# Sliding attention's values: split float32r products against plain float32 products at two column positions

## The chip, the core and the metric

The kernel runs on one core of a Trainium2 chip. The metric is the device time of one execution in microseconds (us), taken as the median of several runs. The engines are named as in the profile: PE is TensorE's matrix product, PEld its load of the stationary operand, DVE is VectorE, ACT is ScalarE, POOL is GpSimd, SP is SyncE, which here only issues DMAs.

## The reference

One layer of a decoder trunk on a sequence of 512 tokens of width 1024, all in float32. The part that matters is the sliding-window attention: eight query heads of width 64, two key and value heads, blocks of 128 queries that see their own block of keys and the one before, ALiBi distances, and a learned sink.

```python
sizes = [SWA_Q, SWA_KV, SWA_KV, DIFF_QK, DIFF_QK, DIFF_V, D_MODEL, D_MODEL]
...
h = _rmsnorm(x, norm1_g[l]) * (1.0 + scale1) + shift1
proj = h @ w_in[l]
qa, ka, va, qd, kd, vd, ga, gd = jnp.split(proj, points, axis=-1)
out_a = _sliding_window_attention(...)     # the part that is changed
out_d = _diff_attention(...)
merged = (jax.nn.sigmoid(ga) * (out_a @ w_branch_swa[l])
          + jax.nn.sigmoid(gd) * (out_d @ w_branch_diff[l]))
x = x + gate1 * (merged @ w_out[l])
...
# in _sliding_window_attention
scores = jnp.einsum('bnqkgd,bnskd->bnkgqs', qb, kb).astype(jnp.float32) * (d ** -0.5)
...
probs = jax.nn.softmax(jnp.concatenate([scores, sink], axis=-1), axis=-1)[..., :-1]
out = jnp.einsum('bnkgqs,bnskd->bnqkgd', probs.astype(v.dtype), vb)
```

A gated MLP with a causal convolution and a final norm follow.

## The kernel before

Every large product is made in three: an operand x is split into a high part, which is x rounded to float32r, and a low part, which is x minus the high part; `mm3` (L119 to L121) multiplies high by high, high by low and low by high and sums them in PSUM. The helper `evac` (L430, L431) makes such a pair out of a PSUM bank: ScalarE copies the high part, then VectorE subtracts it from the bank and writes the low part. The bank is free after the second step.

The stages follow one another: the modulated norm and the projection of queries, keys and values of the sliding attention (to about 60 us), the sliding attention (to about 126 us), the differential attention, the gates and merges, the output projection, and the MLP from about 380 us to the end. PE's order is written out by hand (`manual_schedule`); the orders of VectorE and ScalarE come from a planner that sees priorities (`high_priority`) and dependencies.

The sliding attention works on four pairs of heads. Pair i holds head i, which uses value head 0, and head i + 4, which uses value head 1; j counts the two. For each pair, in PE's order: `swa_scores` (L126: 64 rows of the array for each head, at row positions 0 and 64), `swa_softmax` (L578 exponentials on ScalarE, L586 scaling on VectorE), `swa_transpose` once for each j (L598: seven 128 by 128 transposes, in two banks of the tag "t", and `evac` into pTh and pTl), and `swa_values`. Between these steps `fill(n)` puts n steps of other work on PE, each of three 128x512 products: the projections of the differential heads (pq, pk, pw) and later the gates. Steps of `ada_rows` (L764, tile arow) are put in by the same counter and run on VectorE.

The values are stationary and the transposed probabilities move. `turn_va` (L451) transposes the values of both heads into the bank pva. The stationary tile va has 128 columns for each value head and block: head 0's values stand in columns 0 to 63 and zeros beside them, head 1's in columns 64 to 127 of a second block, so that both heads can add to all 128 rows of one bank. The zeros come from a memset on GpSimd (L436).

```python
nc.gpsimd.memset(va.bitcast(F32), 0.0)
...
for a, cc in ((0, 0), (64, 192)):
    evac(va[:, 0, :, cc : cc + 64], va[:, 1, :, cc : cc + 64], pv3[:, :, a : a + 64])
```

For each j and each of four key blocks kb there is one `mm3`, over 256 columns, or 128 for the last block. The result bank oa is evacuated into outa, which the branch products pA read later.

Plain float32 products occur in two other places: the keep-warm products at the start (L341, 128 by 128 by 128, 14 of them and then three times 3) and reductions over partitions with one moving column (L267, L732).

Of the kernel before, what the change touches and what calls it, by code (L numbers as in the profile page):

```python
# [8 lines left out]
F32 = mybir.dt.float32  # L9
F32R = mybir.dt.float32r  # L10
# [4 lines left out]
P = 128  # L15
# [3 lines left out]
NT = S // P  # L19
# [34 lines left out]
def kernel(  # L54
# [22 lines left out]
    nc = tc.nc  # L77
# [3 lines left out]
    def pool(name, bufs=1, space=None, stack=ctx):  # L81
        kw = {} if space is None else {"space": space}
        return stack.enter_context(tc.tile_pool(name=name, bufs=bufs, reuse_waits="tile", **kw))

    cpool = pool("const")
    big = pool("big")
# [12 lines left out]
    def tbank(name, shape=(P, S)):  # L99
        return bank("t", 2, list(shape), name)  # L100

    def vbank(name):
        return bank("v", 1, [P, S], name)
# [14 lines left out]
    def mm3(o, lh, ll, rh, rl, start, stop):  # L118
        nc.tensor.matmul(o, lh, rh, start=start, stop=False)  # L119
        nc.tensor.matmul(o, lh, rl, start=False, stop=False)  # L120
        nc.tensor.matmul(o, ll, rh, start=False, stop=stop)  # L121
# [35 lines left out]
    rows = cpool.tile([NR, P], F32, name="rows")  # L157
# [264 lines left out]
    ap = pool("att", stack=at)  # L422
    qa = big.tile([P, 4, 2, S], F32R, tag="qa", name="qa")
    ka = big.tile([P, 2, S], F32R, tag="kvA", name="ka")
    va = big.tile([P, 2, 4, 2 * P], F32R, tag="kvB", name="va")
    outa = [big.tile([P, 4, S], F32R, tag=f"out{g}", name=f"outa{g}") for g in "hl"]

    def evac(hi, lo, src, scale=None):
        if scale is None:
            nc.scalar.copy(hi, src)  # L430
            nc.vector.tensor_sub(lo, src, hi.bitcast(F32))  # L431
        else:
            nc.scalar.activation(hi, src, AF.Copy, scale=scale)
            nc.vector.scalar_tensor_tensor(lo, src, scale, hi.bitcast(F32), ALU.mult, ALU.subtract)

    nc.gpsimd.memset(va.bitcast(F32), 0.0)  # L436

    def evac_q(i):
        evac(qa[:, i, 0], qa[:, i, 1], acc6[i], qsc[:, i : i + 1])
# [8 lines left out]
    def turn_va():  # L448
        pv = tbank("pva")
        for t in range(NT):  # L450
            nc.tensor.transpose(pv[:, t * P : (t + 1) * P], vT[:, t * P : (t + 1) * P], ident)  # L451
        pv3 = pv.rearrange("p (t d) -> p t d", t=NT)
        for a, cc in ((0, 0), (64, 192)):
            evac(va[:, 0, :, cc : cc + 64], va[:, 1, :, cc : cc + 64], pv3[:, :, a : a + 64])


    pcv = tbank("pcv", (P, 88))
# [129 lines left out]

    def swa_transpose(i, j):
        c = pairs[i]
        ph = ap.tile([P, 1024], F32R, tag="aTh", bufs=2, name=f"pTh{i}_{j}")  # L590
        pl = ap.tile([P, 1024], F32R, tag="aTl", bufs=2, name=f"pTl{i}_{j}")
        for b in range(2):
            wb = 512 if b == 0 else 384
            tp = tbank(f"tp{i}_{j}_{b}")
            for m in range(wb // P):
                kb, n = 2 * b + m // 2, 2 * b + m // 2 + m % 2
                off = (kb - max(0, n - 1)) * P
                nc.tensor.transpose(tp[:, m * P : (m + 1) * P], c.sb[n][:, j, off : off + P], ident)  # L598
            with tc.high_priority(offset=HP):
                evac(ph[:, b * 512 : b * 512 + wb], pl[:, b * 512 : b * 512 + wb], tp[:, :wb])  # L600
        c.pT.append((ph, pl))

    def swa_values(i):
        o = vbank(f"oa{i}")
        for j in range(2):
            ph, pl = pairs[i].pT[j]
            vs = slice(P * j, P * j + P)
            for kb in (0, 2, 1, 3):
                w = P if kb == 3 else 2 * P
                mm3(  # L610
                    o[:, kb * P : kb * P + w],
                    va[:, 0, kb, vs], va[:, 1, kb, vs],
                    ph[:, kb * 256 : kb * 256 + w], pl[:, kb * 256 : kb * 256 + w],
                    j == 0 and kb == 0, j == 1 and kb == 3,
                )
        evac(outa[0][:, i], outa[1][:, i], o)

# [190 lines left out]
    pairs, firsts, scored, probs, aTs = {}, {}, {}, {}, {}  # L808
# [8 lines left out]
    with tc.issue_after(pairs[0].last.ins):  # L817
        swa_softmax(0)
        fill(1)
        evac_q(3)  # L820
        turn_va()
        fill(SWA_FILL[2] - 1)
    for i in range(SWA_PAIRS):
        more = i + 1 < SWA_PAIRS
        if more:
            swa_scores(i + 1, 0)
        fill(SWA_FILL[3])
        swa_transpose(i, 0)
        fill(SWA_FILL[4])
        swa_transpose(i, 1)  # L830
        if more:
            swa_scores(i + 1, 2)
        fill(SWA_FILL[5])
        if more:
            swa_softmax(i + 1)
        fill(SWA_FILL[6])
        swa_values(i)
        fill(SWA_FILL[7])
# [955 lines left out]
```

## Time and profile before

| what | value |
|---|---|
| median of 3 runs | 716.5 us |
| lowest and highest run | 715.11 and 716.59 us |
| the profiled execution | 716.59 us |
| its span, first to last instruction | 714.5 us |
| mean granted clock of TensorE | 0.993 |

The span lies within the execution; the 2.1 us between them lie around it. In the profile a row of a view names the line, the engine, the operation and the tiles (result, arrow, operands), then the count and the busy time or the durations. In the timeline the first number is the start in us from the start of the span and the second is how long the instruction, or the run of alike instructions, took; a bracket gives how long the engine had been idle and what ended it. Products overlap in PE's pipeline, so the distance from one start to the next, not the duration, is what a product costs.

### The profile page before, as it was taken

Reading aid. Unit: us, or ns where it says so; the run is one execution under the profiler, and the core shown is the slowest. Engines: PE = TensorE matmul, PEld = TensorE weight load, DVE = VectorE, ACT = ScalarE, POOL = GpSimd, SP = SyncE. Lnnn points to the kernel's source line nnn. Section 1 sums busy time; section 2 is a strip of 40 time slices with the busy share of each in tenths; the row PEclk is TensorE's granted clock in tenths of the full one; section 3 lists DMA queues with packets and bytes.
Section 4 is the critical chain, followed back from the end, with each engine's and each line's share of the span. In section 5 each row is a group of like instructions: output and inputs, shape, how many; then the busy total and the mean of one; then the engine's idle time right before and its main releaser. Section 6 shows DMA issues by size and latency. Waiting matters only on the chain. (4 is left out here: it accounts for less than half of the span.)

```text
span 714.5 us, 11275 instructions
## 1 busy us (share of the span) xinstructions
PE 688.4 (96%) x4187; PEld 603.0 (84%) x4187; DVE 588.5 (82%) x1125; ACT 384.2 (54%) x677; POOL 84.4 (12%) x101
## 2 busy tenths in 40 slices
PE   5999899999999999999999999999999999999994
PEld 5777778777787888888879999999999999888884
DVE  5998978797986774865479899888889899979996
ACT  3646566455554233432258666555555666656664
POOL 4000000001000100000012021111111102540300
PEclk9999999999999999999999999999999999999998
DMA  9983522453553664737717598877789738996903
GB/s 307 293 264 96 173 64 83 148 163 102 151 159 105 225 196 140 235 118 210 232 59 148 153 201 203 191 185 217 190 199 229 164 123 233 182 203 194 160 0 119
DMA packets 115863, 121.82 MB, mean 170 GB/s; under 512 B 4415, under 2 KB 93280, under 8 KB 115808
## 3 DMA queue, kind: packets, MB, share of 16 engines
q1 hardware_dynamic: 96894, 95.09, 42.1%
q0 software_dynamic: 18720, 25.73, 21.2%
q8 instruction: 33, 0.54, 0.3%
q10 hardware_dynamic: 194, 0.28, 0.1%
q14 instruction: 22, 0.18, 0.1%
HBM read 118.97 MB, written 2.11 MB: 169 GB/s over the span
## 5 line engine op out<-in xcount | busy, mean ns | idle before, releaser
L1133 PE MATMUL up<-t,m_whi 128*128 128x256 f32 x528 | 96.1, 283 | 0.0
L1133 PEld LDWEIGHTS up<-t,m_whi 128*128 128x128 f32 x528 | 82.3, 192 | 0.0
L1133 PE MATMUL up<-t,m_wlo 128*128 128x256 f32 x264 | 74.7, 283 | 0.1
L1133 PE MATMUL up<-bh,p_wlo 128*128 128x256 f32 x232 | 65.7, 284 | 0.6 <-DVE p_wlo L1076 0.6
L1133 PE MATMUL up<-bh,p_whi 128*128 128x256 f32 x232 | 65.6, 283 | 0.0
L1133 PE MATMUL up<-bl,p_whi 128*128 128x256 f32 x232 | 65.6, 283 | 0.0
L1133 PEld LDWEIGHTS up<-t,m_wlo 128*128 128x128 f32 x264 | 50.6, 192 | 0.3 <-DVE m_wlo L1076 0.3
L1133 PEld LDWEIGHTS up<-bh,p_wlo 128*128 128x128 f32 x232 | 44.4, 192 | 1.1 <-DVE p_wlo L1076 1.1
L1133 PEld LDWEIGHTS up<-bh,p_whi 128*128 128x128 f32 x232 | 44.5, 192 | 0.0
L1133 PEld LDWEIGHTS up<-bl,p_whi 128*128 128x128 f32 x232 | 44.5, 192 | 0.0
L1044 POOL DMA_DIRECT2D s<-in_w_up_dram x21 | 27.2, 1385 | 143.0 <-DMA s<-in_w_up_dram 92.7
L764 DVE SCALAR_TENSOR_TENSOR arow<-ra,cs,arow 128x512 f32<-128x512 f32 x56 | 41.9, 748 | 1.4 <-DMA ra<-in_w_ada_dram 0.7
L1076 DVE TENSOR_TENSOR m_wlo<-s,m_whi 128x1024 fp32r<-128x1024 f32 x31 | 37.7, 1216 | 2.0 <-ACT m_whi L1072 2.0
L1072 ACT CAST m_whi<-s 128x1024 fp32r<-128x1024 f32 x31 | 32.5, 1047 | 9.3 <-DVE s L1066 5.9
L1133 PE MATMUL up<-t,p_whi 128*128 128x256 f32 x176 | 32.2, 283 | 0.0
L175 POOL TENSOR_TENSOR r<-ms,mhalf 128x1 f32<-128x1 f32 (+1 forms) x16 | 13.4, 838 | 144.7 <-DVE ms L173 77.2
L694 ACT ACTIVATE sd<-sd,dmx 128x128 f32<-128x128 f32 (+3 forms) x32 | 17.8, 556 | 22.0 <-DVE dmx L692 15.4
L777 POOL DMA_DIRECT2D mod_rows<-arow x8 | 4.3, 540 | 200.5 <-ACT arow L776 200.3
L1133 PEld LDWEIGHTS up<-t,p_whi 128*128 128x128 f32 x176 | 27.4, 192 | 0.2 <-issue 0.2
L1140 ACT ACTIVATE gT<-a,cv 128x512 f32<-128x512 f32 x22 | 17.7, 813 | 17.6 <-DVE a L1175 17.3
L1072 ACT CAST p_whi<-wa 128x1024 fp32r<-128x1024 f32 x18 | 18.7, 1042 | 12.0 <-PE up L1133 10.8
L1133 PE MATMUL up<-t,p_wlo 128*128 128x256 f32 x88 | 24.9, 283 | 0.0
(485 smaller groups left out, 2119.5 us busy)
## 6 DMA issues: line engine op xcount, KB each, us to landing
ra<-in_w_ada_dram SPq DMA_DIRECT2D x32, 512.0 KB, 4.2
wa<-in_w_up_dram SPq DMA_DIRECT2D x22, 512.0 KB, 4.6
s<-in_w_up_dram SPq DMA_DIRECT2D x21, 512.0 KB, 5.0
s<-in_w_up_dram POOLq DMA_DIRECT2D x21, 512.0 KB, 6.5
adaw<-in_w_ada_dram SPq DMA_DIRECT2D x16, 512.0 KB, 5.1
w<-in_w_in_dram SPq DMA_DIRECT2D x12, 512.0 KB, 3.9
a<-in_w_up_dram SPq DMA_DIRECT2D x11, 512.0 KB, 4.7
b<-in_w_down_dram SPq DMA_DIRECT2D x10, 512.0 KB, 3.9
```

What stands on the lines that cost most here:

```text
L175: nc.gpsimd.tensor_tensor(r0, ms, mhalf[:, :n], ALU.pow)
L694: nc.scalar.activation(pm[m], pm[m], AF.Exp, bias=mx[:, m : m + 1], scale=slope, accum_out=lsum[:, m : m + 1])
L764: nc.vector.scalar_tensor_tensor(ac, r[:, a], cc, ac, ALU.mult, ALU.add)
L777: nc.gpsimd.dma_start(mod_rows[idx : idx + 1, hf * S : (hf + 1) * S], row)
L1044: nc.gpsimd.dma_start(dst, upblock(*blk), accum_op=ALU.add)
L1072: nc.scalar.copy(W[J, name][0], R[J, SRC[name]])
L1076: nc.vector.tensor_sub(lo, R[J, SRC[name]], hi.bitcast(F32))
L1133: nc.tensor.matmul(o[u], w[:, k, cu], b[:, k], start=name in ("p1", "m5", "p2") and k == 0 and x == 0, stop=k == 3 and x == 2, skip_group_ ...
L1140: nc.scalar.activation(grow(j), av[J][:, u], AF.Identity, bias=cv[:, 66 + j : 67 + j], scale=cv[:, 44 + j : 45 + j])
```

## The change

The values of the sliding attention are kept as they are, without a split and without the zeros: va is a float32 tile of 128 columns for each block, one copy out of pva. The transposed probabilities are one float32 tile pT for each head, one copy on ScalarE out of each bank; the low part on VectorE is no longer made. Each product has 64 stationary columns and is a plain float32 product; head j's goes to column position 64 j of the array and to rows 64 j to 64 j + 63 of the bank oa. The loop over the heads is now the inner one. pT takes the buffers of aTh for j = 0 and of aTl for j = 1.

```diff
-    va = big.tile([P, 2, 4, 2 * P], F32R, tag="kvB", name="va")
+    va = big.tile([P, 4, P], F32, tag="kvB", name="va")
...
-    nc.gpsimd.memset(va.bitcast(F32), 0.0)
...
-        pv3 = pv.rearrange("p (t d) -> p t d", t=NT)
-        for a, cc in ((0, 0), (64, 192)):
-            evac(va[:, 0, :, cc : cc + 64], va[:, 1, :, cc : cc + 64], pv3[:, :, a : a + 64])
+        nc.scalar.copy(va, pv.rearrange("p (t d) -> p t d", t=NT))
...
-        ph = ap.tile([P, 1024], F32R, tag="aTh", bufs=2, name=f"pTh{i}_{j}")
-        pl = ap.tile([P, 1024], F32R, tag="aTl", bufs=2, name=f"pTl{i}_{j}")
+        pt = ap.tile([P, 1024], F32, tag="aTh" if j == 0 else "aTl", bufs=2, name=f"pT{i}_{j}")
...
-                evac(ph[:, b * 512 : b * 512 + wb], pl[:, b * 512 : b * 512 + wb], tp[:, :wb])
-        c.pT.append((ph, pl))
+                nc.scalar.copy(pt[:, b * 512 : b * 512 + wb], tp[:, :wb])
+        c.pT.append(pt)
...
         o = vbank(f"oa{i}")
-        for j in range(2):
-            ph, pl = pairs[i].pT[j]
-            vs = slice(P * j, P * j + P)
-            for kb in (0, 2, 1, 3):
-                w = P if kb == 3 else 2 * P
-                mm3(
-                    o[:, kb * P : kb * P + w],
-                    va[:, 0, kb, vs], va[:, 1, kb, vs],
-                    ph[:, kb * 256 : kb * 256 + w], pl[:, kb * 256 : kb * 256 + w],
-                    j == 0 and kb == 0, j == 1 and kb == 3,
-                )
+        for kb in (0, 2, 1, 3):
+            w = P if kb == 3 else 2 * P
+            for j in range(2):
+                rows = slice(64 * j, 64 * j + 64)
+                nc.tensor.matmul(
+                    o[rows, kb * P : kb * P + w], va[:, kb, rows],
+                    pairs[i].pT[j][:, kb * 256 : kb * 256 + w],
+                    start=kb == 0, stop=kb == 3, tile_position=(0, 64 * j),
+                )
```

## The prediction

> **What bounds the kernel now.** I read the page first, for its span and its busy shares, and then its slices, to see whether the stage with the change is like the rest.
>
> ```profile
> span 714.5 us, 11275 instructions
> PE 688.4 (96%) x4187; PEld 603.0 (84%) x4187; DVE 588.5 (82%) x1125; ACT 384.2 (54%) x677; POOL 84.4 (12%) x101
> PE   5999899999999999999999999999999999999994
> DVE  5998978797986774865479899888889899979996
> ```
>
> TensorE is busy 96% of the span, at nine tenths or more in nearly every slice of 17.9 us. Its order is written by hand, so time saved on TensorE early in the kernel stays saved if nothing later is waiting for something else. Next I took windows over the sliding stage, the waits of TensorE over the whole span, and the timeline of TensorE around the places they name.
>
> ```profile
> core 0: us, PE busy (x) PEld busy (x) DVE busy (x) ACT busy (x) POOL busy (x), PEclk, DMA share, GB/s
> 66.00:76.00 10.00, 7.91 (x48) 6.15 (x47) 9.78 (x39) 7.12 (x24) 0.00 (x0) 1.00 0.36 107
> 76.00:86.00 10.00, 10.00 (x68) 8.49 (x66) 9.89 (x26) 6.53 (x23) 0.00 (x0) 1.00 0.48 141
> 86.00:96.00 10.00, 9.19 (x62) 7.21 (x62) 9.93 (x34) 4.83 (x10) 0.00 (x0) 1.00 0.47 147
> 96.00:106.00 10.00, 10.00 (x68) 8.27 (x66) 6.52 (x24) 6.91 (x23) 0.00 (x0) 1.00 0.11 30
> ...
> PE tp L598 <- DVE pTl L431: 2.9, 2, 2.1
> ...
> PE td L709 <- DVE sd L700: 1.8, 4, 1.1
> ```
>
> From 66 to 96 us two engines are full: VectorE 98 to 99%, and TensorE all but the 2.9 us in which the transposes of the probabilities (tp) wait for VectorE's low part (pTl). In the last row only TensorE is full. After the stage the largest wait of TensorE is 1.8 us in all, so what the stage gives or takes should reach the end nearly whole.
>
> **The values' products.** Per pair of heads the kernel before runs 24 products of 128 stationary columns, in float32r. The first pair:
>
> ```profile
> 81.16 0.28 PE L119 MATMUL oa<-pTh,va 128*128 128x256 f32 x1
> 81.27 0.28 PE L120 MATMUL oa<-pTl,va 128*128 128x256 f32 x1
> ...
> 82.29 0.28 PE L120 MATMUL oa<-pTl,va 128*128 128x128 f32 x1
> 82.40 0.27 PE L121 MATMUL oa<-pTh,va 128*128 128x128 f32 x1
> ...
> 83.81 0.27 PE L121 MATMUL oa<-pTh,va 128*128 128x128 f32 x1
> 83.92 0.44 PE L119 MATMUL pw<-hThA,w_h 128*128 128x512 f32 x1
> ```
>
> Starts are what counts, since durations overlap: 0.12 us from one 256-column product to the next, 0.11 for 128 columns, and 83.92 - 81.16 = 2.76 us for the block. Four pairs make 11.0 us.
>
> After it there are 8 products per pair, 4 for each head, three of them over 256 columns and one over 128, in plain float32. What such a product costs must come from the only plain float32 products of the trace, the 23 keep-warm products of the source (14 and three times 3):
>
> ```profile
> L341 PE MATMUL a<-ones,ident 128*128 128x128 f32 x46 | 8.7, 360 | 0.0
> 8.25 1.61 PE L341 MATMUL a<-ones,ident 128*128 128x128 f32 x13
> L598 PE MATMUL tp<-ident,st 128*128 128x128 f32 x56 | 7.8, 277 | 2.9 <-DVE pTl L431 2.9
> ```
>
> 23 products leave 46 records, so each is two instructions. At the full clock 13 of them take 1.61 us; less the last one's own 0.28 that is 1.33 / 12 = 0.111 us a record. So a record of 128 columns costs at most 0.111 us, which is twice what 128 columns need at the rate of the 256-column products. It may be two passes over the columns, or one pass that hides behind the weight load of the next record, as the 0.11 of the 128-column products above does. Two passes make 0.222 us for 256 columns, one makes 0.12. I take two, since 0.111 is what plain float32 was seen to cost and the cheap end needs the load as its excuse. The Trainium skill, FP8 and Floating Point Precision, TensorE Precision Notes, has four passes for a true float32 product, two for each record; by it the sum is the same, and the cheap end falls away.
>
> One after another the 16 records of a pair are 12 x 0.222 + 4 x 0.111 = 3.11 us. The second question is whether the two column positions run beside each other. The nearest row is the scores, which use two row positions (64 rows each):
>
> ```profile
> 85.59 0.39 PE L120 MATMUL pw<-hTlA,w_h 128*128 128x512 f32 x1
> 85.82 0.40 PE L121 MATMUL pw<-hThA,w_l 128*128 128x512 f32 x1
> 86.14 0.95 PE L126 MATMUL sw<-ka,qa 64*128 64x128 f32 x12
> 87.03 0.50 PE L119 MATMUL pw<-hThA,w_h 128*128 128x512 f32 x1
> 87.37 0.40 PE L120 MATMUL pw<-hTlA,w_h 128*128 128x512 f32 x1
> ```
>
> Twelve products end within 0.95 us; less the last one's 0.28 that is 0.67 us, where eleven steps of 0.11 to 0.12 would take 1.21 to 1.32. So two row positions run together. Columns differ, because both heads then read all 128 partitions at once; I take them to run together all the same, as the nearest row. Each head's two records must follow each other, so the second head starts one record late: 3.11 / 2 + 0.11 = 1.67 us. The Trainium skill, TensorE: Matmul & The Clock Gate, Measured speedup vs the span model, gives 2.38 times for three column positions of 32; no run here shows columns, and the sum does not need it.
>
> Changing the shape of the array also costs. The 512-column products step by 0.23 us (85.59 to 85.82), so the next could start at 86.05, and the one before 87.37 counts as if started at 87.14. The scores' block thus takes 1.09 us, of which six steps, of two products each at 0.11 to 0.12, are 0.69; in and out cost 0.40. I charge this to each values block, now 1.67 + 0.40 = 2.07 us: 0.69 less than 2.76, four times, **2.8 us saved**. One pass without running together gives 12 x 0.12 + 4 x 0.06 = 1.68, the same block, so the forecast needs only one of the two halvings. The bounds are 1.68 / 2 + 0.12 + 0.40 = 1.36 us (both) and 3.51 us (neither): from 5.6 saved to 3.0 lost.
>
> **The waits.** Each transposed block had two evacuations, and its bank came free after the second:
>
> ```profile
> 72.06 0.60 PE L598 MATMUL tp<-ident,st 128*128 128x128 f32 x4
> ...
> 73.14 0.58 ACT L430 CAST pTh<-tp 128x512 fp32r<-128x512 f32 x1
> ...
> 74.01 0.69 DVE L431 TENSOR_TENSOR pTl<-tp,pTh 128x512 fp32r<-128x512 f32 x1
> ...
> 74.76 0.55 PE L598 MATMUL tp<-ident,st 128*128 128x128 f32 x3 [2.09 <-DVE pTl L431]
> ...
> 89.24 0.97 ACT L430 CAST pTh<-tp 128x512 fp32r<-128x512 f32 x2 [0.86 <-PE tp L598]
> ...
> 90.47 0.40 PE L121 MATMUL pw<-hThB,w_l 128*128 128x512 f32 x1
> ...
> 91.68 0.44 PE L598 MATMUL tp<-ident,st 128*128 128x128 f32 x2 [0.81 <-DVE pTl L431]
> ```
>
> The change drops the VectorE step. In the built order the second half of the first transposes then waits for the ScalarE copy of va instead of pTl; that copy stands where the first half of va's evacuation stood, at 67.1 us, some 5 us before it is needed. So the 2.09 us go. The next transposes, at 90.47 + 0.23 = 90.70, need the bank whose ScalarE copies end at 89.24 + 0.97 = 90.21, so the 0.81 us go as well. With the ramp at each restart the starts are 74.76 - 72.06 = 2.70 us apart where four transposes take four steps of 0.11, and 1.21 us apart where 0.23 is normal: 2.26 + 0.98 = **3.2 us saved**. What is late next is the same copy: the second head's transposes come after the first's seven and two fills of three products, at 72.06 + 7 x 0.11 + 6 x 0.23 = 74.2 us, and need the bank copied from 73.14 on and the one behind it, done at about 74.2. That is the same moment, so 0 to 1 us of new wait stays open.
>
> **VectorE and the rest.** From the tile views of the probabilities and of va:
>
> ```profile
> L119 PEld LDWEIGHTS oa<-pTh,va x32: 187/192/192, 80.9 to 124.5; 128*128 128x128 f32 x32
> ...
> L431 DVE TENSOR_TENSOR pTl<-tp,pTh x16: 544/620/692, 74.0 to 122.1; 128x512 fp32r<-128x512 f32 x8, 128x384 fp32r<-128x384 f32 x8
> L431 DVE TENSOR_TENSOR va<-pva,va x2: 414/415/416, 68.0 to 74.6; 128x256 fp32r<-128x256 f32 x2
> L430 ACT CAST va<-pva x2: 351/362/373, 67.1 to 71.5; 128x256 fp32r<-128x256 f32 x2
> L436 POOL MEMSET va<- x1: 1802/1802/1802, 4.7 to 4.7; 128x2048 f32 x1
> ```
>
> VectorE loses 16 x 0.62 + 2 x 0.415 = 10.8 us. Only the waits above turn into time: from 96 us on VectorE has room, and its 10.8 us are slack under it. They keep VectorE from becoming the bound when TensorE is 6 us sooner. ScalarE does one copy of 512 columns (about 0.58 us, as the 0.58 of pTh) for two of 0.36, and 16 copies as before; at 48 to 71% busy in the windows above both are covered. The memset of 1.8 us on GpSimd (12% busy) goes for nothing, as TensorE's first use of va is at 81 us. Weight loads on the DMA queues keep their order.
>
> **The sum.** The profiled execution took 716.59 us (span 714.5 and 2.1 around it): 716.59 - 2.8 - 3.2 = 710.6. The median of the runs is 716.5, so **710.5 us**.
>
> **The rivals.**
>
> *Column positions one after another.* If the two heads cannot stream at once, a block is 3.11 + 0.40 = 3.51 us, 0.75 more than now: 4 x 0.75 = 3.0 lost, 3.2 won, 716.3: no change. For it: no record here has two streams over the same partitions. Against it: the scores' pairs. Chance 0.25, own range 715 to 718.
>
> *Both halvings.* Together and one pass: 716.5 - 5.6 - 3.2 = 707.7. Against it, the 0.111 us. Chance 0.08.
>
> *Exposed weight loads (slower).* Each record needs a load of its own, 16 per pair, where now the next load runs under the product (a load is 0.19 us long, by the first row of the last fence, while starts are 0.12 apart). If loads to one position cannot run under the other's product, each record pays in addition the step of a load, 0.11 us for 128 columns, perhaps half for 64: 3.11 + 0.40 + 16 x 0.055 = 4.39 us, 1.63 more, 6.5 lost less 3.2 won: 719.8; with whole loads 723.3. It decides from a block of 2.76 + 3.2 / 4 = 3.56 us on. For it: two records per product and short streams. Against it: in the rows above loads hide under products in one position. The Trainium skill, TensorE: Matmul & The Clock Gate, What overlaps and what doesn't, says that a load overlaps a running product only where the row groups differ. Both positions use all rows, so by it this rival would come; the trace disagrees for full-width products, which all use all rows. Chance 0.15.
>
> *The waits come back.* If the transposes arrive 3 us sooner only to wait for L586 or for the copy, the 2.8 alone stays: 713.7. Against it: VectorE's 10.8 us. Chance 0.10.
>
> **How the numbers follow.** The forecast has what is left, 0.42. Its own range is 709 to 712.5. Two tenths may be left out: the slower rival and half of the fast one, 0.15 + 0.04, so the range goes from 707.5 to 718.0. A change under 0.2% (1.4 us) can't be told from none here, that is 715.1 to 717.9. Faster: 0.42 + 0.10 + 0.08, and 0.02 of the second case, 0.62. Slower: 0.15 and 0.03 of it, 0.18. Same: 0.20.
>
> **What would show it.** Right: 64 records of the values' line; the first to the last start of a block about 1.6 us, block in all 2.1; no wait of tp for VectorE; the stage's end near 6 us earlier, and that difference the same at 300 us and at the end. Wrong: a block of 3 us or more (serial, or loads in the gaps between), tp waiting for pT or st, or a difference that shrinks after 130 us.

## The result and the profile after

The changed kernel takes 708.41 us (median; 706.73 to 709.57), the kernel before 716.31 us beside it. The ratio is 0.9891 with a 95% interval of 0.9868 to 0.9914, that is 6.1 to 9.5 us less; the forecast was 710.5 us. The profiled execution took 708.24 us, with a span of 705.4.

The page of the changed kernel, its busy shares and two of its slice rows:

```profile
span 705.4 us, 11197 instructions
PE 685.0 (97%) x4155; PEld 597.1 (85%) x4155; DVE 578.4 (82%) x1107; ACT 383.9 (54%) x676; POOL 82.2 (12%) x100
PE   6999999999999999999999999999999999999994
DVE  5998968788985766773579899888888999979996
```

TensorE loses 3.4 us of busy time, VectorE 10.1. The windows over the sliding stage:

```profile
66.00:76.00 10.00, 10.00 (x68) 8.07 (x67) 9.90 (x34) 7.94 (x25) 0.00 (x0) 1.00 0.35 107
76.00:86.00 10.00, 10.00 (x64) 7.46 (x63) 9.09 (x30) 7.58 (x24) 0.00 (x0) 1.00 0.80 254
86.00:96.00 10.00, 10.00 (x72) 7.49 (x70) 7.14 (x32) 7.19 (x24) 0.00 (x0) 1.00 0.24 63
96.00:106.00 10.00, 10.00 (x70) 7.80 (x68) 6.92 (x28) 6.32 (x18) 0.00 (x0) 1.00 0.19 53
```

The first column after the window's length is PE: the 2.1 us missing from 66 to 76 us before, and the 0.8 from 86 to 96, are gone. VectorE is full now only up to 76 us, and at nine tenths up to 86. The waits of TensorE no longer name tp; the largest of the attention stages is the one in the differential attention:

```profile
PE td L702 <- DVE sd L693: 1.6, 3, 1.1
```

The timeline of TensorE, first around the two transposes of the first pair and then around its values block:

```profile
71.31 0.93 PE L593 MATMUL tp<-ident,st 128*128 128x128 f32 x7
71.99 0.48 PE L119 MATMUL pk<-hThA,w_h 128*128 128x512 f32 x1
...
73.47 0.93 PE L593 MATMUL tp<-ident,st 128*128 128x128 f32 x7
74.32 0.39 PE L126 MATMUL sw<-ka,qa 64*128 64x256 f32 x2
```

```profile
77.89 0.39 PE L121 MATMUL pw<-hThA,w_l 128*128 128x512 f32 x1
78.21 1.73 PE L604 MATMUL oa<-pT,va 128*64 128x256 f32 x16
79.87 0.50 PE L119 MATMUL pw<-hThA,w_h 128*128 128x512 f32 x1
80.21 0.40 PE L120 MATMUL pw<-hTlA,w_h 128*128 128x512 f32 x1
```

Both groups of seven transposes run without a break. The block goes from 78.21 to 79.87 us, 1.66, where it was 2.76. Counted with its changes of shape, as the prediction counted the scores' block, it lasts from 77.89 + 0.23 = 78.12 to 80.21 - 0.23 = 79.98: 1.86 us. The block before, counted so, lasted from 81.16 to 84.20 - 0.23 = 83.97 (the 84.20 is the start of the second pw product after it): 2.81. So a block saves 0.95 us. The fourth block saves a little more: right behind it stand the scores of the differential attention (tile sd), which use row positions too. Block and scores together took from 122.19 to 126.27 - 0.23 = 126.04 us, 3.85, and now take from 114.83 + 0.23 = 115.06 to 118.04 - 0.23 = 117.81, 2.75: 1.10 less. In all the blocks save 3 x 0.95 + 1.10 = 3.95 us.

The tile view of oa, and the windows of the products of oa alone in steps of about 0.22 us (the count in brackets is of the records under way in the stretch):

```profile
L604 PEld LDWEIGHTS oa<-pT,va x64: 132/137/138, 78.2 to 116.5; 128*64 128x64 f32 x64
L604 PE MATMUL oa<-pT,va x64: 272/379/430, 78.2 to 116.6; 128*64 128x256 f32 x48, 128*64 128x128 f32 x16
```

```profile
core 0: us, PE busy (x), PEclk, DMA share, GB/s
78.20:78.47 0.27, 0.26 (x2) 1.00 1.12 341
78.47:78.69 0.22, 0.22 (x4) 1.00 1.15 356
78.69:78.90 0.21, 0.21 (x4) 1.00 1.22 424
```

Two records are under way from the very start, one of each head, and every later stretch of 0.215 us sees two end and two begin. So a record of 256 columns costs 0.215 us, nearly twice the 0.12 of a float32r product, as two passes would, and the two column positions run together with no lag between the heads.

### The profile page after: what moved, and what is told of

Its sections match the earlier page's. It is cut to its first block, busy times and chain, and to the rows that moved or that the text cites. A ratio compares the mean times of both kernels' runs of the same rounds, so it can differ in the third digit from the quotient of the medians.

```text
span 705.4 us, 11197 instructions
## 1 busy us (share of the span) xinstructions
PE 685.0 (97%) x4155; PEld 597.1 (85%) x4155; DVE 578.4 (82%) x1107; ACT 383.9 (54%) x676; POOL 82.2 (12%) x100
```

## The experiments

All comparisons are with the kernel before, run beside the kernel in question; times are medians.

**The order of the products.** The two heads run together although each head's two records must follow each other. Is it the order, or does each position take its own records?

```diff
-        for kb in (0, 2, 1, 3):
-            w = P if kb == 3 else 2 * P
-            for j in range(2):
+        for j in range(2):
+            for kb in (0, 2, 1, 3):
```

> The changed kernel with the two loops of the values' products exchanged: all four products of head 0 (column position 0), then all four of head 1 (position 64). Theory A, each position takes its next product when its own columns are free: the two heads still run together, a values block keeps its 1.86 us, the time stays at 708.4 us. Theory B, TensorE starts products strictly in program order and the two run together only because neighbours in the order lie at different positions: the heads run one after the other, a block takes about 3.0 + 0.35 us, 1.5 us more, four times: 714.4 us.

710.24 us, ratio 0.9918 (0.9892 to 0.9944). Neither theory holds. The timeline, and two tile views of oa, up to 79.14 us and up to 79.2 us:

```profile
78.23 2.65 PE L604 MATMUL oa<-pT,va 128*64 128x256 f32 x16
80.81 0.50 PE L119 MATMUL pw<-hThA,w_h 128*128 128x512 f32 x1
```

```profile
L604 PE MATMUL oa<-pT,va x4: 379/379/430, 78.2 to 78.9; 128*64 128x256 f32 x4
```

```profile
L604 PE MATMUL oa<-pT,va x6: 379/379/431, 78.2 to 79.2; 128*64 128x256 f32 x6
```

A block takes 80.81 - 78.23 = 2.58 us, 0.92 more than 1.66, and not the 1.5 more of theory B. Four records of head 0 run alone; with its fifth, head 1's first starts, although three records of head 0 stand ahead of it in the program. That is how it would go if each position had a queue of its own, with one record running and about three waiting, and the program order held up the other position only when a fifth must wait. One common window that looks about four records ahead would give the same; no run here parts the two. Four steps of 0.215 us are 0.86, close to the 0.92 lost. Over four blocks that is 3.7 us, as the trace has it (the last product of oa starts at 120.3 us instead of 116.6); the ratios differ by less, about 1.9 us, but each is known only to about 1.8 us either way.

**How far ahead a record can start.** The products in groups of two for each head, four records:

```diff
+        for kbs in ((0, 2), (1, 3)):
+            for j in range(2):
+                for kb in kbs:
```

> The changed kernel with the values' products in groups of two for each head (four records at one column position, then four at the other). Theory, TensorE takes up to four records of one position, one running and three waiting, before the program order blocks: groups of four records then run together as well as groups of two, a block keeps its 1.66 us from its first start to the next product's, the time about 708.2 us. Rival, any longer group delays the other head in proportion, as the groups of eight did by 0.92 us: about 0.4 us more per block, 709.8 us.

707.87 us, ratio 0.9891 (0.9853 to 0.9928).

```profile
78.37 1.78 PE L605 MATMUL oa<-pT,va 128*64 128x256 f32 x16
80.09 0.50 PE L119 MATMUL pw<-hThA,w_h 128*128 128x512 f32 x1
```

1.72 us instead of 1.66: nearly nothing is lost, as the theory has it. The trace decides here; with two executions, the interval of the ratio covers the rival's time too.

**Without column positions.** The zeros of the kernel before, in plain float32:

```diff
+    va = big.tile([P, 4, 2 * P], F32, tag="kvB", name="va")
+    nc.gpsimd.memset(va, 0.0)
...
+        for j in range(2):
+            for kb in (0, 2, 1, 3):
...
+                    o[:, kb * P : kb * P + w], va[:, kb, P * j : P * j + P],
```

> The changed kernel with the zero-padded values of the kernel before, in plain float32 without splits: 8 products per pair of 128 stationary columns, no column positions, both heads into all 128 rows. The evacuation stays the changed kernel's (one ScalarE copy). Theory, the two column positions halve the streaming: 16 records one after another, 12 x 0.216 + 4 x 0.108 = 3.02 us with no change of the array's shape, against 1.86 us: 1.16 us more per block, 4.6 in all, 713.0 us. Rival, the gain comes from VectorE's relief and the waits, and the products' shape hardly counts: 708.4 us.

712.86 us, ratio 0.9963 (0.9946 to 0.9980).

```profile
79.20 0.39 PE L121 MATMUL pw<-hThA,w_l 128*128 128x512 f32 x1
79.43 3.19 PE L606 MATMUL oa<-pT,va 128*128 128x256 f32 x16
82.38 0.48 PE L119 MATMUL pw<-hThA,w_h 128*128 128x512 f32 x1
```

The block takes 2.95 us, against 2.76 for the 24 float32r products. Plain float32 alone is thus a small loss on TensorE; that this kernel is still 2.7 us faster than before goes with the waits, which it does not have either. The column positions are worth the other 5 us, about. The rival falls. (The copy of va is made in two halves here, not in one as the expectation says.)

**Twice the products.** To part the streaming from the changes of shape:

```diff
+        for rep in range(2):
             for kb in (0, 2, 1, 3):
```

> The changed kernel with every values block made twice over, the second time from the start, so the second pass gives the result. Theory, changing the array's shape costs about 0.35 us once per block: the second pass costs the streaming alone, 1.51 us, four times 6.0: 714.4 us. Rival, the cost lies in each product (a fixed part per record) and not in the change of shape: 1.86 us more per block, 7.4 in all: 715.8 us. The distance of the starts in the trace decides where the times are too close.

713.36 us, ratio 0.9969 (0.9955 to 0.9984).

```profile
78.45 3.25 PE L605 MATMUL oa<-pT,va 128*64 128x256 f32 x32
81.63 0.50 PE L119 MATMUL pw<-hThA,w_h 128*128 128x512 f32 x1
```

81.63 - 78.45 = 3.18 us, 1.52 more than 1.66. The second pass costs six steps of 0.215 and two of 0.108 and nothing else; that is the theory's price and not the rival's 1.86. The remaining 1.86 - 1.51 = 0.35 us of a block is paid once, for going in and out. It goes with the shape of the array and not with the data type: at full width the first plain float32 product starts 0.23 us after the float32r product before it (79.20 to 79.43), which is that product's normal step.

**The low parts put back.** First VectorE's subtraction for the transposes alone, then that of va as well:

```diff
                 nc.scalar.copy(pt[:, b * 512 : b * 512 + wb], tp[:, :wb])
+                low = va4[:, 1 + b].rearrange("p t d -> p (t d)")
+                nc.vector.tensor_sub(low[:, :wb], tp[:, :wb], pt[:, b * 512 : b * 512 + wb])
```

> The changed kernel with VectorE's low part of each transposed block put back (the subtraction is made, read from the bank, and its result is read by nobody), so that a bank of the transposes is free only after VectorE again. Theory, the waits of the transposes for VectorE were worth 3.2 us: 711.6 us, with waits of tp for that subtraction in the trace. Rival, the waits were a matter of va's evacuation or of the values block alone: 708.4 us.

709.54 us, ratio 0.9907 (0.9876 to 0.9937), between the two forecasts, and TensorE's waits in the sliding stage:

```profile
PE tp L594 <- DVE va L598: 2.3, 3, 0.8
```

(The subtraction writes into a spare part of va's tile, hence the name.) The waits are back, but in three pieces of at most 0.8 us: the first, of 2.1 us, is missing.

```diff
+        for a in (0, 64):
+            h = slice(a, a + 64)
+            nc.scalar.copy(va[:, :, h], pv3[:, :, h])
+            nc.vector.tensor_sub(va4[:, 3, :, h], pv3[:, :, h], va[:, :, h])
```

> The changed kernel with all of VectorE's low parts put back, those of the transposed blocks and those of va in two halves as before (made and read by nobody), so that what is left of the change is the values' products alone. Theory, the missing part of the first wait belongs to va's evacuation: the first transposes wait about 2 us again, the second about 1 us, 3.2 us in all, 711.2 us. Rival, the wait of 2.1 us came from the transposes' own low part alone: no more than with that part put back, 709.5 us.

712.89 us, ratio 0.9955 (0.9941 to 0.9970).

```profile
71.32 0.60 PE L598 MATMUL tp<-ident,st 128*128 128x128 f32 x4
74.02 0.55 PE L598 MATMUL tp<-ident,st 128*128 128x128 f32 x3 [2.10 <-DVE va L602]
74.32 0.53 PE L119 MATMUL pk<-hThA,w_h 128*128 128x512 f32 x1
74.65 0.63 PE L120 MATMUL pk<-hTlA,w_h 128*128 128x512 f32 x1
75.07 0.63 PE L121 MATMUL pk<-hThA,w_l 128*128 128x512 f32 x1
```

VectorE at the same time:

```profile
73.27 0.69 DVE L602 TENSOR_TENSOR va<-tp,pT 128x512 f32<-128x512 f32 x1
73.88 0.41 DVE L455 TENSOR_TENSOR va<-pva,va 128x256 f32<-128x256 f32 x1
```

The 2.1 us are back. So the first wait needs both subtractions. The one for va's second half (L455) stands in VectorE's order behind the one for the first transposed block (L602), so by these times the bank pva is still held when that block is done; as the tag has two banks, the second half of the transposes must use the first half's, and starts at 74.02 us, when L602 is through (73.27 + 0.69 = 73.96). What is left of the change in this kernel, the products alone, is 2.1 to 4.2 us by the interval, in line with the 3.95 of the trace. The time is above the theory's 711.2 us, which the interval (711.3 to 713.4) just leaves out; with the blocks' measured 3.95 us alone it would be 711.6, which lies inside.

**The memset.** The change dropped the zeros and with them the memset on GpSimd. Put back:

```diff
+    nc.gpsimd.memset(outa[0].bitcast(F32), 0.0)
```

> The changed kernel with the memset of 2048 float32 columns on GpSimd put back at its old place in GpSimd's queue (it zeroes outah, which is written later anyway). Theory: the memset holds up VectorE's three small operations on cols (1.0 to 1.2 us instead of 0.17), but their result waits for the weights' DMA anyway, so the time stays within 0.2 us of the changed kernel's, about 708 us. Rival: it is what made the start 0.7 us later in the kernel before: 708.7 us, and ScalarE's first square (L351) starts at 9.2 us instead of 8.1 to 9.1.

706.80 us, ratio 0.9877 (0.9848 to 0.9906): no cost, and ScalarE's first square starts at 8.33 us, so the rival falls. That is so though VectorE's small operations last until the memset ends:

```profile
4.71 1.80 POOL L427 MEMSET outah<- 128x2048 f32 x1
...
5.48 1.05 DVE L243 TENSOR_SCALAR cols<-cols 128x8 f32<-128x8 f32 x1
...
6.70 0.61 DVE L256 TENSOR_SCALAR ac<-adaw,cs 128x256 f32<-128x256 f32 x2
```

**The values next to the scores.** Each values block moved behind the fill that followed it, in front of the next scores:

```diff
         fill(SWA_FILL[6])
-        swa_values(i)
         fill(SWA_FILL[7])
+        swa_values(i)
```

> The changed kernel with each values block moved behind its following fill of three steps, so that it stands right in front of the next scores, which use two row positions. Theory, a change of shape costs its 0.35 us per visit because the array drains, so going from column positions straight to row positions saves one of two drains three times: 0.5 us less in the trace, about 707.7 us, not to be told apart by times. Rival, going from one split shape to the other costs as much as going through the full shape: nothing saved in the trace, 708.2 us.

706.46 us, ratio 0.9879 (0.9848 to 0.9910). The ratio cannot be told from the changed kernel's; the trace can.

```profile
79.31 0.39 PE L121 MATMUL pw<-hThA,w_l 128*128 128x512 f32 x1
79.63 1.74 PE L604 MATMUL oa<-pT,va 128*64 128x256 f32 x16
81.30 0.96 PE L126 MATMUL sw<-ka,qa 64*128 64x128 f32 x12
82.18 0.50 PE L119 MATMUL pw<-hThA,w_h 128*128 128x512 f32 x1
82.52 0.40 PE L120 MATMUL pw<-hTlA,w_h 128*128 128x512 f32 x1
```

From 79.31 + 0.23 = 79.54 to 82.52 - 0.23 = 82.29 the two blocks take 2.75 us, where apart they take 1.86 + 1.09 = 2.95. One change of shape less saves 0.2 us. The expectation counted three such places; there are two, since behind the third block no scores are left in the stage and a fill follows it as before. That makes 0.4 us. The fourth block stands in front of scores in the changed kernel already:

```profile
115.15 1.73 PE L604 MATMUL oa<-pT,va 128*64 128x256 f32 x16
116.82 0.95 PE L126 MATMUL sd<-qkv 64*128 64x128 f32 x12
```

This kernel has the lowest median of all that were run, but by less than the scatter of its executions.

## Why the prediction was right

*The bound.* TensorE's time passed on whole. The last product of oa starts at 124.8 us before and at 116.6 after, 8.2 us apart; the last gate product of the differential attention (pgd), at about 320 us, is about 8.5 apart, and the spans differ by 9.1. The difference does not shrink.

*The values' products.* Right in kind, too small in size: 0.69 us a block was forecast, 0.95 came (1.10 for the fourth), 3.95 in all for 2.8. The term that was wrong is "the second head starts one record late": 0.11 us were charged for a lag that isn't there. The first record of the second head starts with that of the first, ahead of a record that stands before it in the program, as the head-outer order showed to be possible. The rest of the difference is small: 0.215 for 0.222 us a record, 0.35 for the 0.40 of the shape, and 0.05 us of ramp that the block before had behind it too. That only one of the two halvings takes place was right: two passes, and both heads at once. The Trainium skill, FP8 and Floating Point Precision, TensorE Precision Notes, with its four passes for a float32 product, agrees with two records of 0.215 us each, nearly two steps of 0.12 in each record.

*The waits.* 3.2 us forecast; the two waits before are gone in the trace, and putting back what caused them brings 3.3 us of waits back. By the starts in the timelines the first was worth 2.3 us (the two heads' transposes start at 72.06 and 76.53 us before, at 71.31 and 73.47 after) and the second 1.1 us (from the first head's transposes to the scores behind the second's: 88.55 to 92.62 before, 84.52 to 87.53 after). The same stretch of the third pair is 0.2 us shorter as well, which makes 3.5 in all. The cause given for the first was incomplete: the prediction named pTl, and it was pTl with va's second evacuation holding the other bank. The 0 to 1 us of new wait left open did not come: the second transposes start at 73.47 us, seven steps after the first and two fills later, with no wait.

*VectorE and the rest.* As forecast, the 10.8 us of VectorE are slack beyond the waits: with the full-width products, where VectorE is relieved and the block is 0.2 us dearer, the gain shrinks to 1.4 to 3.9 us. The memset is free.

*The sum.* The blocks' 3.95 and the waits' 3.5 make 7.5 us where 6.0 were forecast; the medians say 7.9, and 6.1 to 9.5 by the interval. The two traces differ by 9.1 us. Of the 1.6 left, 0.7 stands before anything changed: ScalarE's first square waits for the DMA that brings x, and starts at 9.24 us before and 8.55 after. The first transposes of x follow at 12.62 and 11.93 us; in the other kernels' traces they start between 11.55 and 12.44, with and without the memset. So it is probably scatter of the start and not the change, though only one trace of the kernel before is there to judge by. Another 0.6 arises in the MLP's norm (tile th, 367 to 382 us), where TensorE waits 1.3 us for VectorE before and 0.7 after; that wait lies between nothing and 1.8 us in the other traces, so it is not put down to the change either. What makes up the last 0.3 was not tried.

*How close it was.* The measured 708.41 us lies below the forecast's own range of 709 to 712.5. It lies within the whole range only because that was drawn down to 707.5 for the rival of both halvings, which did not come true; that much was luck. The parts say more for the forecast than the number: each step came, and the forecast savings were 1.15 and 0.3 us too small.

*The rivals.* Positions one after another: its price was 3.11 us of streaming for a block, and the full-width kernel, where the records do follow one another, measured 2.95; here it did not happen. Both halvings: excluded by 0.215 us a record. Exposed loads: the rule of the Trainium skill, TensorE: Matmul & The Clock Gate, What overlaps and what doesn't, by which loads overlap products only across row groups, is not what these traces show; 16 loads of 0.137 us, all over the same 128 rows, lie in a block of which 1.51 us are streaming and 0.35 the change of shape, and doubling the block added no more than its streaming. The waits coming back: not in the changed kernel.

## What to carry to other kernels

Two products with half the stationary columns can share the array at two column positions, and a dearer but unsplit data type may then still win, as it takes a whole evacuation step off another engine. Count the passes and the positions separately, charge each visit to another array shape once, and put such visits next to each other. And where a transpose waits for its bank, look for every reader of every bank of that tag, not only for the last one named.

## What the runs showed of the hardware beyond what was expected

A record at one column position can start ahead of records of the other position that stand before it in the program, as long as no more than about three of those are waiting; past that the program order holds it up (0.92 us lost with eight records in a row, 0.06 with four).

A change of array shape costs 0.35 to 0.40 us for in and out together, and going from column positions straight to row positions saves 0.2 of it.

A wait of 2.1 us on TensorE can cost more than itself. In the profiled execution with all low parts put back, the products after it step by 0.42 us instead of 0.23 (74.65 to 75.07), and the window there has a lower clock:

```profile
74.00:78.00 4.00, 3.98 (x15) 0.58 0.04 13
```

The 0.58 is the granted clock. In the kernel before, the same wait left it at 1.00 (74 to 78 us of its trace); what makes the difference was not tried. Nor was it tried whether some of the scatter of 1 to 2 us between executions of one kernel comes from such windows; this execution, at 714.32 us, was the slowest of its kernel's ten, whose median is 712.89. The Trainium skill, TensorE: Matmul & The Clock Gate, Part 1: The HAM clock gate, has the clock at half after an idle window of about 3.4 us, until a busy window as long has passed. The length agrees, as a clock of 0.58 over 4 us is 3.4 us at half; the idle time does not, as 2.1 us were enough here.
